# SwiGLU weights split partly by transfers: a negated copy and an adding transfer for the low halves of the output weights, a rounding transfer for the high halves of the up weights

## The chip, the cores and the metric

The kernel runs on one core of a Trainium2 chip. The metric is the device time of one execution in microseconds (us). A core has five engines with instruction queues of their own: TensorE (PE; its weight loads are listed as PEld), VectorE (DVE), ScalarE (ACT), GpSimd (POOL) and SyncE (SP), which here only issues transfers. Each engine takes its instructions in the order of its queue; semaphores order the engines among each other. Sixteen DMA engines move data between DRAM and the on-chip memory.

## The reference

Four layers of a decoder trunk on 512 tokens of 1024 features. Each layer is a token mixer followed by a SwiGLU channel mixer; the change touches the latter alone.

```python
def swiglu(h, w_in, w_out):
    gu = h @ w_in
    return (jax.nn.silu(gu[..., :FFN_HIDDEN]) * gu[..., FFN_HIDDEN:]) @ w_out

for i in range(DEPTH):
    mod = einsum('bd,sde->sbe', silu(c), ada_w[i]) + ada_b[i][:, None, :]
    shift, scale, gate = split(mod, 3, axis=-1)
    ...
    h = x * (1 + scale[1][:, None]) + shift[1][:, None]
    y = swiglu(h, ffn_w_in[i], ffn_w_out[i])
    x = layer_norm(ALPHA * x + (1 + gate[1][:, None]) * y, ln_g[i, 1], ln_b[i, 1])
```

FFN_HIDDEN is 2816, everything is float32. `mod` is the conditioning: columns of scale, shift and gate for each sublayer.

## The kernel before

All activations lie as [feature, token]; a product is a tile of 128 output features by 512 tokens in one bank of PSUM (there are 8 banks). TensorE works in a one-pass format with a shorter mantissa (float32r), so each float32 operand is kept as a high half (the value rounded to that format) and a low half (the rest), and a product is three matmuls: high by high, high by low, low by high (`mm3`, L188 to L190). Tiles of high and low halves of weights are called `wh` and `wl`, those of the modulated input `hh` and `hl`, those of activations `b` in the profile (`b4`, `b2` in the instruction lists).

`weights` brings one tile of weights: SP loads the float32 values into a `raw` tile (L175), ScalarE copies them rounded into `wh` (L178), VectorE writes `wl` = raw - wh (L179). There are five buffers of raw, five of `wh` and five of `wl`. After each weight load, `weights` calls `ada_steps`, which takes one column of the conditioning of a later sublayer from a list: SP loads 512 KB of `ada_w` into a raw tile (L111), VectorE multiplies it with the condition and sums it (L112, one long instruction and a short read of the sum). In a SwiGLU stage the first ten weight loads have no such step (`hold`), and there are 48 of them in each of the first three layers' stages, none in the last.

A SwiGLU stage (`ffn`) goes through the 22 tiles of hidden features in groups of 7, 7 and 8 (FGROUPS). In each group `proj_cols` makes the gate and the up tile of each hidden tile (weights of 512 KB, gate first; the first two hidden tiles of the stage run together in two halves of the tokens), and `gated` makes the activation: silu on ScalarE (L420), times the up tile on VectorE (L421), high half on ScalarE (L422), low half on VectorE (L423). Then `out_proj` multiplies the group's activations with eight output weights (448 KB each, 512 KB in the third group), and `fold` adds each of the eight tiles to the residual `xz` on VectorE (L305). In the third group fold also sums for LayerNorm (L310 to L316), four of its tiles run in two halves of the tokens, and the products that come next begin behind LayerNorm of the first half. `layer_norm` and `modulate` give the next input, with GpSimd computing h (L406). The output projections of the mixers use the same `out_proj`, with two output tiles for each weight load (per = 2); the SwiGLU's have per = 1.

The order on each engine's queue follows from the order in which the program is written and from a scheduler that places each instruction by it; nothing is sorted by hand here.

Of the kernel before, what the change touches and what calls it, by code (L numbers as in the profile page):

```python
# [10 lines left out]
F32 = mybir.dt.float32  # L11
# [3 lines left out]
AF = mybir.ActivationFunctionType  # L15
ALU = mybir.AluOpType
# [3 lines left out]
P = 128  # L20
# [16 lines left out]
# order in which the first input (a) and the first projection (w) are issued  # L37
# [3 lines left out]
class Trunk:  # L41
# [65 lines left out]
    # Output features lie on partitions, so that a product and its sum are one instruction.  # L107
    # They run in steps between the weight loads (see weights()).
# [30 lines left out]
    # The first sublayer's input, one feature tile at a time; its gate comes later.  # L139
# [29 lines left out]
    def weights(self, src, n, eng=None):  # L169
        nc = self.nc  # L170
        raw = self.raw.tile([P, D], F32, tag="raw", name=self.nm("raw"))
        dst = raw[:, :n]
        if len(src.shape) == 3:
            dst = dst.rearrange("p (a b) -> p a b", a=src.shape[1])
        nc.sync.dma_start(dst, src)  # L175
        hi = self.wp.tile([P, D], F32R, tag="wh", name=self.nm("wh"))
        lo = self.wp.tile([P, D], F32R, tag="wl", name=self.nm("wl"))
        nc.scalar.activation(hi[:, :n], raw[:, :n], AF.Copy)  # L178
        (eng or nc.vector).tensor_tensor(lo[:, :n], raw[:, :n], hi[:, :n].bitcast(F32), ALU.subtract)  # L179
        if self.hold:  # L180
            self.hold -= 1
        else:
            self.ada_steps(self.rate)
        return hi, lo
# [17 lines left out]
    def merge(self, *procs):  # L202
        """procs: (generator, total); advances the one that is furthest behind"""
# [10 lines left out]
    def pipeline(self, units, skew):  # L214
        """stage s of unit i comes at step i + skew[s], older units first"""
# [7 lines left out]
    def proj_cols(self, srcs, split, done):  # L223
        """tiles of 128 features: [feature, token]; done(list of banks);
        split: "t" in two halves of the tokens, "k" one input tile at a time"""
        ws = []
        for i, x in enumerate(srcs):
            ws.append(self.weights(x, D, self.nc.gpsimd if split == "k" and i in (1, 3) else None))
            if split == "k":
                yield 0.0  # L230
# [29 lines left out]
    def proj_tok(self, src, n, done):  # L260
        """[token, n features], a bank per 128 tokens; src: [128, 8, n] in DRAM; done(tt, bank)"""
# [24 lines left out]
    def out_proj(self, srcs, per, acts, gate, last):  # L286
        """srcs: one DRAM source for every `per` tiles of 128 output features;
        acts: [128, 2, T] hi/lo tiles. The last group also sums for LayerNorm and
        does `half` of the tiles in two halves of the tokens."""
# [29 lines left out]
        for d0 in range(0, KD - halves, per):  # L319
            w = self.weights(srcs[d0 // per], per * n * P)  # L320
# [5 lines left out]
        if last:  # L326
            ds = list(range(KD - halves, KD))
            ws = {d: self.weights(srcs[d // per], per * n * P) for d in ds[::per]}
# [11 lines left out]
    def layer_norm(self, sub, nxt, half):  # L340
# [3 lines left out]
        # per-token sums as columns, [token, (S1, S2), 2 blocks of tokens]  # L344
# [14 lines left out]
        # back to rows on every partition  # L359
# [32 lines left out]
    # the residual of the next sublayer  # L392
# [17 lines left out]
    def ffn(self, layer, gate):  # L410
        nc, a = self.nc, self.a
        j0 = 0
        for gi, gn in enumerate(FGROUPS):
# [13 lines left out]
            while j < j0 + gn:  # L427
                m = 2 if (gi == 0 and j == 0) else 1
                srcs = [a["ffn_in"][layer, jj, :, x, :] for jj in range(j, j + m) for x in range(2)]
                yield from self.proj_cols(srcs, "t" if m == 2 else None, gated)  # L430
# [7 lines left out]
    def out_srcs(self, w, half):  # L438
        """two output tiles per load, input features of one half"""
# [10 lines left out]
    def transpose_out(self, ytok, n, acts):  # L450
        """ytok: [128 tokens, 4, n*128] -> n hi/lo tiles [128 features, 2, T]"""
# [12 lines left out]
    # x ** -0.5 on a small tile  # L464
# [136 lines left out]
    # 0 where key s <= query t (s on partitions), NEG elsewhere  # L601
# [42 lines left out]
    def rope(self, dst, ps, tt, nh):  # L644
        """dst [128, nh*64] <- rotated ps"""
# [11 lines left out]
    # [keys, queries] masks added to scores: 0 where lo <= q - key < hi, else NEG  # L657
# [254 lines left out]
    def hgrn(self, layer, gate):  # L912
# [79 lines left out]
        def mix(hd):  # L992
# [17 lines left out]
            for l in range(NL + 2):  # L1010
                # K: k times the decay to the end of its block of h, Q: q times the decay
                # from the start of its block, B: the decay over each block
# [92 lines left out]
    def run(self, plan):  # L1105
        """plan: [(kind, layer)] sublayers, sub = 2*layer + (kind == 'ffn')"""
# [5 lines left out]
        for i, (kind, layer) in enumerate(plan):  # L1112
# [15 lines left out]
            # the second half of the tokens is normalised behind the first products  # L1128
# [32 lines left out]
    # alternates so that both end together  # L1161
# [83 lines left out]
```

## Time and profile before

| | |
|---|---|
| median of 2 runs | 2500.31 us (2499.88 to 2500.74) |
| span of the profiled execution | 2498.0 us |
| SwiGLU stages, from and to | 256 to 627, 797 to 1168, 1480 to 1852, 2113 to 2484 us |
| first SwiGLU stage: gate and up tiles | 256 to 339, 378 to 454, 493 to 580 us |
| first SwiGLU stage: output projections | 339 to 378, 454 to 493, 580 to 627 us |

The profile shows one execution. Its span runs from the first to the last instruction; the time of a run is 2.3 us longer than this span. A row of the page's groups reads: line, engine, operation, output and inputs, shapes, count, then busy time and mean of one, then the engine's idle time just before such instructions and what ended it. A row of the list of waits reads: engine, what it wrote and the line, the instruction waited for, then total us, times, the longest. A row of the timeline reads: start, length, engine, line, operation, tiles, and in brackets the idle time before. The landing time of a transfer is counted from its issue to its data being there.

### The profile page before, as it was taken

Reading aid. Unit: us, or ns where it says so; the run is one execution under the profiler, and the core shown is the slowest. Engines: PE = TensorE matmul, PEld = TensorE weight load, DVE = VectorE, ACT = ScalarE, POOL = GpSimd, SP = SyncE. Lnnn points to the kernel's source line nnn. Section 1 sums busy time; section 2 is a strip of 40 time slices with the busy share of each in tenths; the row PEclk is TensorE's granted clock in tenths of the full one; section 3 lists DMA queues with packets and bytes.
Section 4 is the critical chain, followed back from the end, with each engine's and each line's share of the span. In section 5 each row is a group of like instructions: output and inputs, shape, how many; then the busy total and the mean of one; then the engine's idle time right before and its main releaser. Section 6 shows DMA issues by size and latency. Waiting matters only on the chain.

```text
span 2498.0 us, 34328 instructions
## 1 busy us (share of the span) xinstructions
PE 2446.3 (98%) x12920; PEld 2052.5 (82%) x12920; DVE 1432.3 (57%) x2743; ACT 916.6 (37%) x1685; POOL 478.4 (19%) x716
## 2 busy tenths in 40 slices
PE   5999999999999999999999999999999999999998
PEld 4788888888768888889888898888888888888887
DVE  6955765544687655646555566656465556433334
ACT  3433522223653422233433334222345554422223
POOL 7002200003334000104433340000052224000002
PEclk9999999999999999999999999999999999999999
DMA  7842466642211566632222125666422111333331
GB/s 273 287 158 78 132 203 198 198 154 84 77 51 49 171 203 191 206 118 76 77 68 66 63 68 179 205 189 203 119 68 85 60 60 45 109 100 93 101 93 34
DMA packets 93973, 311.94 MB, mean 125 GB/s; under 512 B 10736, under 2 KB 13168, under 8 KB 93808
## 3 DMA queue, kind: packets, MB, share of 16 engines
q1 hardware_dynamic: 92800, 309.43, 38.5%
q8 instruction: 101, 1.65, 0.3%
q10 hardware_dynamic: 1008, 0.32, 0.1%
q14 instruction: 64, 0.52, 0.1%
HBM read 307.62 MB, written 2.10 MB: 124 GB/s over the span
## 4 chain that ended last, share of the span: by engine, by line
PE 89%; DVE 5%; POOL 3%; issue 1%; ACT 1%; DMA 0%; ACTq 0%; POOLq 0%; DVEq 0%
PE ps L188 26%; PE ps L190 26%; PE ps L189 26%; POOL h L406 1%; PE ps L1019 1%; PE ps L853 1%; PE ps L715 1%; DVE wl L179 1%; PE ps L1080 1%; PE ps L881 1%; DVE xz L373 1%; PE ps L746 1%; PE ps L562 1%; DVE xz L381 1%; DVE hl L407 1%
## 5 line engine op out<-in xcount | busy, mean ns | idle before, releaser
L178 ACT ACTIVATE wh<-raw 128x1024 fp32r<-128x1024 f32 (+1 forms) x395 | 410.4, 1042 | 1051.5 <-PE ps L189 652.0
L188 PE MATMUL ps<-hh,wh 128*128 128x512 f32 (+1 forms) x1768 | 655.8, 374 | 19.2 <-ACT wh L178 16.2
L190 PE MATMUL ps<-hh,wl 128*128 128x512 f32 (+1 forms) x1768 | 658.0, 373 | 6.0 <-POOL wl L179 5.1
L189 PE MATMUL ps<-hl,wh 128*128 128x512 f32 (+1 forms) x1768 | 657.4, 373 | 3.7 <-POOL hl L407 3.3
L179 DVE TENSOR_TENSOR wl<-raw,wh 128x1024 fp32r<-128x1024 f32 (+1 forms) x393 | 488.6, 1246 | 284.9 <-ACT wh L178 261.7
L188 PE MATMUL ps<-b,wh 128*128 128x512 f32 (+1 forms) x1216 | 428.0, 352 | 0.0
L189 PE MATMUL ps<-b,wh 128*128 128x512 f32 (+1 forms) x1216 | 421.6, 347 | 0.0
L190 PE MATMUL ps<-b,wl 128*128 128x512 f32 (+1 forms) x1216 | 421.0, 346 | 0.0
L188 PEld LDWEIGHTS ps<-hh,wh 128*128 128x128 f32 x1768 | 333.9, 189 | 76.6 <-ACT wh L178 16.2
L190 PEld LDWEIGHTS ps<-hh,wl 128*128 128x128 f32 x1768 | 334.5, 189 | 65.4 <-POOL wl L179 5.8
L189 PEld LDWEIGHTS ps<-hl,wh 128*128 128x128 f32 x1768 | 334.7, 189 | 64.4 <-POOL hl L407 4.6
L112 DVE CUSTOM_DVE_ANT_0 raw<-raw,cond,adab 128x1024 f32<-128x1024 f32 x192 | 252.2, 1317 | 196.3 <-DMA raw<-in_ada_w 193.2
L188 PEld LDWEIGHTS ps<-b,wh 128*128 128x128 f32 x1216 | 228.7, 188 | 33.4 <-issue 1.2
L189 PEld LDWEIGHTS ps<-b,wh 128*128 128x128 f32 x1216 | 228.6, 188 | 32.9 <-issue 2.0
L190 PEld LDWEIGHTS ps<-b,wl 128*128 128x128 f32 x1216 | 228.5, 188 | 31.0
L305 DVE SCALAR_TENSOR_TENSOR xz<-ps,gate,xz 128x512 f32<-128x512 f32 (+1 forms) x208 | 129.8, 625 | 193.0 <-PE ps L190 192.5
L188 PE MATMUL ps<-wh,hh 128*128 128x512 f32 (+1 forms) x608 | 237.4, 393 | 2.5 <-ACT wh L178 1.5
L189 PE MATMUL ps<-wl,hh 128*128 128x512 f32 (+1 forms) x608 | 221.5, 364 | 0.6 <-DVE wl L179 0.6
L190 PE MATMUL ps<-wh,hl 128*128 128x512 f32 (+1 forms) x608 | 221.6, 365 | 0.0
L421 DVE TENSOR_TENSOR b<-ps,b 128x512 f32<-128x512 f32 x88 | 60.4, 690 | 142.0 <-PE ps L190 139.1
L188 PEld LDWEIGHTS ps<-wh,hh 128*128 128x128 f32 x608 | 115.0, 189 | 23.4 <-issue 3.2
L189 PEld LDWEIGHTS ps<-wl,hh 128*128 128x128 f32 x608 | 115.1, 189 | 19.6 <-DVE wl L179 2.2
(253 smaller groups left out, 2384.1 us busy)
## 6 DMA issues: line engine op xcount, KB each, us to landing
raw<-in_ada_w SPq DMA_DIRECT2D x192, 512.0 KB, 4.1
raw<-in_ffn_in SPq DMA_DIRECT2D x176, 512.0 KB, 3.6
raw<-in_ffn_out SPq DMA_DIRECT2D x64, 448.0 KB, 3.4
raw<-in_ffn_out SPq DMA_DIRECT2D x32, 512.0 KB, 3.5
raw<-in_m_vo SPq DMA_DIRECT2D x16, 512.0 KB, 5.2
raw<-in_h_qf SPq DMA_DIRECT2D x16, 512.0 KB, 3.3
raw<-in_h_ig SPq DMA_DIRECT2D x16, 512.0 KB, 3.9
raw<-in_d_qk SPq DMA_DIRECT2D x16, 512.0 KB, 3.9
```

The source lines that it names most:

```text
L112: self.nc.vector.tensor_tensor_reduce(w, w, self.cond, 1.0, self.adab[:, sub, j : j + 1], ALU.mult, ALU.add, mod[:, j : j + 1])
L178: nc.scalar.activation(hi[:, :n], raw[:, :n], AF.Copy)
L179: (eng or nc.vector).tensor_tensor(lo[:, :n], raw[:, :n], hi[:, :n].bitcast(F32), ALU.subtract)
L188: nc.tensor.matmul(ps, lhs[0], rhs[0], start=start, stop=False)
L189: nc.tensor.matmul(ps, lhs[0], rhs[1], start=False, stop=False)
L190: nc.tensor.matmul(ps, lhs[1], rhs[0], start=False, stop=stop)
L305: nc.vector.scalar_tensor_tensor(z, ps[:, t], gate[:, d : d + 1], z, ALU.mult, ALU.add)
L373: V.tensor_tensor(z, z, st[:, 0, :], ALU.subtract)
L381: V.tensor_tensor(z, z, st[:, 1, :], ALU.mult)
L406: nc.gpsimd.tensor_scalar(h, z, hs[:, k : k + 1], hb[:, k : k + 1], ALU.mult, ALU.add)
L407: (eng or nc.vector).tensor_tensor(self.hl[:, k, t], h, self.hh[:, k, t].bitcast(F32), ALU.subtract)
L421: nc.vector.tensor_tensor(s, pu, s, ALU.mult)
```

## The change

`weights` gets a parameter `how`. With "cast" (the up weights, every second one of `proj_cols` in `ffn`) the high half is written by a transfer that GpSimd issues straight from DRAM, rounding on its way, instead of by ScalarE; raw is still loaded and VectorE still subtracts. With "add" (the output weights of the SwiGLU) ScalarE makes the high half as before, then writes the negated, rounded value into `wl`, and a transfer issued by GpSimd adds the float32 weights from DRAM to it; VectorE's subtraction is gone. There are 88 weights of the first kind (22 hidden tiles, 4 layers) and 96 of the second (64 of 448 KB, 32 of 512 KB). The rest of the diff takes comments out and moves line numbers by 9 from there on.

```diff
-    def weights(self, src, n, eng=None):
+    def weights(self, src, n, eng=None, how=None):
...
-        nc.scalar.activation(hi[:, :n], raw[:, :n], AF.Copy)
-        (eng or nc.vector).tensor_tensor(lo[:, :n], raw[:, :n], hi[:, :n].bitcast(F32), ALU.subtract)
+        if how == "cast":
+            nc.gpsimd.dma_start(hi[:, :n], src)
+        else:
+            nc.scalar.activation(hi[:, :n], raw[:, :n], AF.Copy)
+        if how == "add":
+            nc.scalar.activation(lo[:, :n], raw[:, :n], AF.Copy, scale=-1.0)
+            nc.gpsimd.dma_start(lo[:, :n], src, accum_op=ALU.add)
+        else:
+            (eng or nc.vector).tensor_tensor(lo[:, :n], raw[:, :n], hi[:, :n].bitcast(F32), ALU.subtract)
...
-    def proj_cols(self, srcs, split, done):
+    def proj_cols(self, srcs, split, done, how=None):
...
-            ws.append(self.weights(x, D, self.nc.gpsimd if split == "k" and i in (1, 3) else None))
+            eng = self.nc.gpsimd if split == "k" and i in (1, 3) else None
+            ws.append(self.weights(x, D, eng, how if i % 2 else None))
...
-            w = self.weights(srcs[d0 // per], per * n * P)
+            w = self.weights(srcs[d0 // per], per * n * P, how="add" if per == 1 else None)
...
-            ws = {d: self.weights(srcs[d // per], per * n * P) for d in ds[::per]}
+            ws = {d: self.weights(srcs[d // per], per * n * P, how="add" if per == 1 else None) for d in ds[::per]}
...
-                yield from self.proj_cols(srcs, "t" if m == 2 else None, gated)
+                yield from self.proj_cols(srcs, "t" if m == 2 else None, gated, "cast")
```

In the new numbering the rounding transfer is L180, the high half on ScalarE L182, the negated copy L184, the adding transfer L185 and the subtraction L187. Numbers behind a tile's name count tiles and instructions and differ between the two programs.

GpSimd's queue where the first SwiGLU stage begins, before; sq and S belong to the sums for LayerNorm, lnv is its reciprocal root, h the next input.

```order
L310 TENSOR_SCALAR S_93<-xz_90 128x256
L316 TENSOR_TENSOR S_93<-S_93,sq_334_1909 128x256
L466 TENSOR_TENSOR lnv_337_1919<-lnv_337_1919,mhalf_101 128x2
L316 TENSOR_TENSOR S_93<-S_93,sq_339_1939 128x256
L316 TENSOR_TENSOR S_93<-S_93,sq_341_1957 128x256
L406 TENSOR_SCALAR h_343_1970<-xz_90,hs_303_1706,hb_304_1707 128x256
L316 TENSOR_TENSOR S_93<-S_93,sq_345_1988 128x256
L406 TENSOR_SCALAR h_346_1994<-xz_90,hs_303_1706,hb_304_1707 128x256
```

And after; wh_365 and wh_371 are the stage's first two up weights.

```order
L319 TENSOR_SCALAR S_93<-xz_90 128x256
L180 DMA wh_365_2096<-in_ffn_in 128x1024
L325 TENSOR_TENSOR S_93<-S_93,sq_334_1909 128x256
L475 TENSOR_TENSOR lnv_337_1919<-lnv_337_1919,mhalf_101 128x2
L325 TENSOR_TENSOR S_93<-S_93,sq_339_1939 128x256
L325 TENSOR_TENSOR S_93<-S_93,sq_341_1957 128x256
L415 TENSOR_SCALAR h_343_1970<-xz_90,hs_303_1706,hb_304_1707 128x256
L180 DMA wh_371_2108<-in_ffn_in 128x1024
L325 TENSOR_TENSOR S_93<-S_93,sq_345_1988 128x256
L415 TENSOR_SCALAR h_346_1994<-xz_90,hs_303_1706,hb_304_1707 128x256
```

The two rounding transfers stand between the sums and the tiles of h; each waits there until TensorE has released its buffer.

VectorE's queue at the turn from the gate and up tiles of the first group to its output projection, before; b4_445 is the group's last activation, the L112 rows are conditioning steps.

```order
L112 ISA raw_480_2943,mod_359_2086<-raw_480_2943,cond_94,adab_97 128x1024
L112 ISA mod_359_2086 128x1
L421 TENSOR_TENSOR b2_446_2740<-ps_444_2690,b2_446_2740 128x512
L179 TENSOR_TENSOR wl_469_2876<-raw_467_2873,wh_468_2875 128x896
L423 TENSOR_TENSOR b4_445_2739<-b2_446_2740,b4_445_2739 128x512
L112 ISA raw_485_2975,mod_359_2086<-raw_485_2975,cond_94,adab_97 128x1024
L112 ISA mod_359_2086 128x1
L305 SCALAR_TENSOR_TENSOR xz_90<-ps_451_2754,gate_302_1705,xz_90 128x512
L179 TENSOR_TENSOR wl_474_2908<-raw_472_2905,wh_473_2907 128x896
L112 ISA raw_490_3007,mod_359_2086<-raw_490_3007,cond_94,adab_97 128x1024
L112 ISA mod_359_2086 128x1
```

And after, where the fold is L314.

```order
L112 ISA raw_480_2950,mod_359_2086<-raw_480_2950,cond_94,adab_97 128x1024
L112 ISA mod_359_2086 128x1
L430 TENSOR_TENSOR b2_446_2740<-ps_444_2690,b2_446_2740 128x512
L112 ISA raw_485_2983,mod_359_2086<-raw_485_2983,cond_94,adab_97 128x1024
L112 ISA mod_359_2086 128x1
L432 TENSOR_TENSOR b4_445_2739<-b2_446_2740,b4_445_2739 128x512
L314 SCALAR_TENSOR_TENSOR xz_90<-ps_451_2755,gate_302_1705,xz_90 128x512
L112 ISA raw_490_3015,mod_359_2086<-raw_490_3015,cond_94,adab_97 128x1024
L112 ISA mod_359_2086 128x1
L314 SCALAR_TENSOR_TENSOR xz_90<-ps_456_2788,gate_302_1705,xz_90 128x512
```

The subtractions for the output weights are gone, and the conditioning step on raw_485 now stands ahead of the last activation's low half (L432, before L423) instead of behind it.

ScalarE's queue at the same turn, before.

```order
L178 ACTIVATE wh_463_2843<-raw_462_2841 128x896
L420 ACTIVATE b2_446_2740<-ps_443_2689 128x512
L178 ACTIVATE wh_468_2875<-raw_467_2873 128x896
L422 ACTIVATE b4_445_2739<-b2_446_2740 128x512
L178 ACTIVATE wh_473_2907<-raw_472_2905 128x896
```

And after.

```order
L182 ACTIVATE wh_463_2846<-raw_462_2844 128x896
L429 ACTIVATE b2_446_2740<-ps_443_2689 128x512
L184 ACTIVATE wl_464_2847<-raw_462_2844 128x896
L182 ACTIVATE wh_468_2879<-raw_467_2877 128x896
L184 ACTIVATE wl_469_2880<-raw_467_2877 128x896
L431 ACTIVATE b4_445_2739<-b2_446_2740 128x512
L182 ACTIVATE wh_473_2912<-raw_472_2910 128x896
L184 ACTIVATE wl_474_2913<-raw_472_2910 128x896
```

Behind each high half of an output weight stands the negated copy of the same weight; two of these copies (wl_464, wl_469) now stand ahead of the last activation's high half (L431, before L422). The orders of SP's queue are the same in both, a weight load and a conditioning load in turns, and TensorE's differ only in a few places just behind the start of each SwiGLU stage.

## The prediction, made before the changed kernel was run

> **What bounds the kernel now.** I read the page from the top: the busy line, the slices, and the chain that ended last.
>
> ```profile
> span 2498.0 us, 34328 instructions
> PE 2446.3 (98%) x12920; PEld 2052.5 (82%) x12920; DVE 1432.3 (57%) x2743; ACT 916.6 (37%) x1685; POOL 478.4 (19%) x716
> DMA  7842466642211566632222125666422111333331
> PE 89%; DVE 5%; POOL 3%; issue 1%; ACT 1%; DMA 0%; ACTq 0%; POOLq 0%; DVEq 0%
> ```
>
> TensorE is busy for 98% of the span and carries 89% of the chain. VectorE, from which the change takes most, is busy 57% and carries 5%. Next the waits of TensorE, and what each SwiGLU stage holds (length; then PE, PEld, DVE, ACT and POOL busy with their counts; clock, share of the 16 DMA engines, GB/s).
>
> ```profile
> PE ps L188 <- ACT wh L178: 17.7, 3, 16.2
> PE ps L190 <- POOL wl L179: 5.1, 1, 5.1
> 256.00:627.00 371.00, 369.45 (x1812) 311.15 (x1811) 214.90 (x319) 116.04 (x154) 37.53 (x47) 1.00 0.52 162
> 797.00:1168.00 371.00, 370.12 (x1810) 312.43 (x1809) 217.11 (x322) 116.83 (x153) 50.84 (x81) 1.00 0.51 162
> 1480.00:1852.00 372.00, 370.47 (x1816) 312.08 (x1816) 216.52 (x312) 117.33 (x155) 36.28 (x46) 1.00 0.51 162
> 2113.00:2484.00 371.00, 369.21 (x1811) 311.13 (x1809) 151.18 (x209) 112.57 (x149) 29.57 (x34) 1.00 0.27 85
> ```
>
> The two largest waits hold single pieces of 16.2 and 5.1 us; they are the first projection of the program, which the change leaves alone. In the four stages that it touches TensorE lacks 1.55, 0.88, 1.53 and 1.79 us of the stage's length, 5.8 us in all. That is the most that any gain can bring. What can be lost is not bounded by such a row, so the rest is about losses. The clock is 1.00 throughout and the same matmuls stay, so I let it out of the sum.
>
> **The change, part by part.** Means by form (count | busy, mean ns | idle before, releaser):
>
> ```profile
> L178 ACT ACTIVATE wh<-raw 128x1024 fp32r<-128x1024 f32 x331 | 349.3, 1059 | 811.5 <-PE ps L189 511.0 <-issue 227.8 <-PE ps L190 43.6
> L178 ACT ACTIVATE wh<-raw 128x896 fp32r<-128x896 f32 x64 | 61.0, 954 | 240.1 <-PE ps L189 141.0 <-issue 99.1
> L179 DVE TENSOR_TENSOR wl<-raw,wh 128x1024 fp32r<-128x1024 f32 x329 | 418.8, 1276 | 248.8 <-ACT wh L178 227.6 <-PE ps L190 18.0
> L179 DVE TENSOR_TENSOR wl<-raw,wh 128x896 fp32r<-128x896 f32 x64 | 69.8, 1091 | 36.1 <-ACT wh L178 34.1
> L112 DVE CUSTOM_DVE_ANT_0 raw<-raw,cond,adab 128x1024 f32<-128x1024 f32 x192 | 252.2, 1317 | 196.3 <-DMA raw<-in_ada_w 193.2
> ```
>
> *Arithmetic.* VectorE loses the low halves of the 96 output weights: 64 x 1.091 + 32 x 1.276 = 110.7 us. ScalarE loses the high halves of the 88 up weights, 88 x 1.059 = 93.2, and gains 96 negated copies, 64 x 0.954 + 32 x 1.059 = 94.9: no change. Neither sets the end here. ScalarE's copies wait for TensorE to give buffers back (511.0 us of idle time before them), that is, weights stand ready. All this is worth 0.
>
> *Transfers.* GpSimd issues 184 more, 88 x 512 + 64 x 448 + 32 x 512 KB, about 90 MB. What the engines now carry (same columns as the stages; 339 to 378 is an output projection, 378 to 454 the gate and up tiles behind it, 2196 to 2235 the same projection in the last layer, which loads no conditioning):
>
> ```profile
> 339.00:378.00 39.00, 39.00 (x168) 31.37 (x168) 23.82 (x31) 8.55 (x10) 1.81 (x4) 1.00 0.65 203
> 378.00:454.00 76.00, 76.00 (x337) 62.91 (x336) 43.79 (x57) 21.22 (x28) 0.23 (x1) 1.00 0.63 194
> 2196.00:2235.00 39.00, 39.00 (x170) 31.58 (x169) 15.89 (x18) 8.75 (x10) 0.00 (x0) 1.00 0.32 108
> ```
>
> Eight plain loads of 448 KB cost 0.32 x 39 = 12.5 us of the DMA engines, 1.56 each. With eight adding ones at the plain price the loaded projection goes from 0.65 to 0.97. TensorE's pace is 39 / 8 = 4.88 us an output weight and 76 / 14 = 5.43 an input weight, and with five buffers a new one has 4 x 4.88 = 19.5 us. The longer way of a low half (two copies of 0.954, then issue and transfer) leaves the last two 17.6 us. So a single added transfer is hidden; what it does to its neighbours need not be.
>
> *The chain of conditioning loads.* In these stages SP alternates weight load and conditioning load. Each conditioning load waits until VectorE's L112 is done with the previous one, and L112 stands in VectorE's queue between the folds and the activations. Three rows of that instruction (the 1st, 8th and 23rd from there on), the end of one and the load issued on it, the landing times in the windows 338:378 and 378:454, and the median landings of other loads (KB, us):
>
> ```profile
> 341.36 1.28 DVE L112 CUSTOM_DVE_ANT_0 raw<-raw,cond,adab 128x1024 f32<-128x1024 f32 x1
> 378.32 1.28 DVE L112 CUSTOM_DVE_ANT_0 raw<-raw,cond,adab 128x1024 f32<-128x1024 f32 x1 [1.83 <-DMA raw<-in_ada_w]
> 457.04 1.28 DVE L112 CUSTOM_DVE_ANT_0 raw<-raw,cond,adab 128x1024 f32<-128x1024 f32 x1 [0.37 <-DMA raw<-in_ada_w]
> 529.86 1.28 DVE L112 CUSTOM_DVE_ANT_0 raw<-raw,cond,adab 128x1024 f32<-128x1024 f32 x1 [1.05 <-DMA raw<-in_ada_w]
> 338.02 0.08 DVE L112 DVE_READ_ACCUMULATOR2_ANT mod<- 128x1 f32 x1
> 338.13 0.33 SPq L111 DMA_DIRECT2D raw<-in_ada_w  x1
> DMA to landing us min/median/max: 3.2/3.5/4.4
> DMA to landing us min/median/max: 3.3/3.8/4.4
> raw<-in_ffn_in SPq DMA_DIRECT2D x176, 512.0 KB, 3.6
> raw<-in_m_vo SPq DMA_DIRECT2D x16, 512.0 KB, 5.2
> ```
>
> In the projection a step of this chain takes (378.32 - 341.36) / 7 = 5.28 us: 3.5 landing, 1.36 for L112 and its read, 0.42 between. TensorE needs 4.88 a step, so VectorE falls 8 x 0.40 = 3.2 us behind. In the next fourteen steps it takes (457.04 - 378.32) / 15 = 5.25 against 5.43 and makes 14 x 0.18 = 2.5 us good. The chain is level with TensorE by a hair, and whatever lengthens a landing is added to each step.
>
> All three transfers of a step are released by the same event, the end of an output tile on TensorE (the fold, then L112 and the next conditioning load; the two copies, then the weight load and the adding transfer), so they share the DMA engines. At the plain price an adding transfer puts between nothing and its whole 1.56 us ahead of the conditioning load; I take the middle, 0.8, so 3.5 becomes 4.3 and the step 6.08: 8 x (6.08 - 4.88) = 9.6 us behind. In the input stage every other step has a rounding transfer of 1.56 x 512 / 448 = 1.8 us; half of it every second step is 0.45, and the step between 5.25 (hidden in waits for TensorE) and 5.70: between 2.5 us made good and 3.8 lost; I take the middle, 0.6 lost.
>
> Where TensorE meets it is the next turn from gate and up to output projection. There L112 now stands ahead of the last activation's low half:
>
> ```profile
> 340.61 0.68 DVE L423 TENSOR_TENSOR b<-b,b 128x512 fp32r<-128x512 f32 x1
> 343.02 0.39 PE L189 MATMUL ps<-b,wh 128*128 128x512 f32 x1
> ```
>
> That half was done at 341.29 and is needed at 343.02. Behind L112 (341.36 + 1.36 + 0.68) it is done at 343.40: 0.4 us late at the first turn, with nothing else changed. At the second turn it is late by 0.4 + 9.6 + 0.6 less the 0.4 already waited: 10.2. At the third the conditioning has ended (last L112 at 529.86, turn at 580), and VectorE has caught up. So 10.6 us a layer, and three layers load conditioning: 31.8 us. Ends: 3 x 0.4 = 1.2 (no landing grows) and 3 x (8 x 1.96 + 3.8 + 0.4) = 60 (all of a plain transfer in front).
>
> *Start of each SwiGLU stage.* The second up weight of the stage gets its buffer late, and its high half now needs a transfer where a copy stood:
>
> ```profile
> 253.24 1.06 ACT L178 ACTIVATE wh<-raw 128x1024 fp32r<-128x1024 f32 x1 [0.26 <-PE ps L189]
> 256.93 0.28 PE L188 MATMUL ps<-hh,wh 128*128 128x256 f32 x1
> 248.90 0.83 POOL L466 TENSOR_TENSOR lnv<-lnv,mhalf 128x2 f32<-128x2 f32 x1
> 253.06 0.73 POOL L316 TENSOR_TENSOR S<-S,sq 128x256 f32<-128x256 f32 x1 [0.36 <-ACT sq L314]
> ```
>
> From 253.24 to 256.93 are 3.69 us. The trace has no transfer issued by GpSimd; its instruction on two columns, 0.83, is the nearest row for a fixed cost, and the landing is 3.6: 0.74 us late, 4 x 0.74 = 3.0 us for four layers. Ends: 0, and with 5.2 for the landing 4 x 2.34 = 9.4. Behind this issue GpSimd's queue holds a sum for LayerNorm (here 253.06) and the next tiles of h; with 0.8 us for the issue they move by less than they idle. The Trainium skill ("DMA: Bandwidth & Descriptors", Latency and other measured facts) gives about 1 us to the first byte on GpSimd's path and 0.6 on SP's; by this estimate the delay would be 0.4 instead of 0.83 and the term 1.2 us; no run so far shows it.
>
> Sum: 2498.0 + 31.8 + 3.0 = 2532.8 us of span. The median of the runs, 2500.31, lies 2.3 us above the profiled span; with it 2535 us.
>
> **The rivals.** *Hidden* (no landing grows): 2498.0 + 1.2 + 3.0 + 2.3 = 2504 to 2505. For it: in the projection landings spread only from 3.2 to 4.4 at a share of 0.65. Against it: the share goes to 0.97.
>
> *The adding transfer costs twice a plain one or more* (other side of the line). It must read what it adds to. At 3.12 us each, half in front makes the landing 5.06 and the step 6.84: 3 x (15.7 + 0.6 + 0.4) = 50 us, 2553; all in front, 6.62 and 8.40: 3 x (28.2 + 3.8 + 0.4) = 97, 2600; the middle is 2577. The projection would then need 25.4 + 25 us of the DMA engines in 39, so they fall behind too. The line of 2%, 2550, is crossed when the landing in the projection reaches 4.95 us instead of 3.5. For it: 5.2 us under the load of the start, where the slices show 7 and 8 tenths. Against it: there many loads stand in one queue, here three. The Trainium skill ("Collectives: The Full Stack", Part 3: Why 7× under link rate — side-by-side accounting) has such a rule: an add in the DMA issues two source reads for each chunk where a copy issues one, on the same ring, and ran at 1/1.93 of the rate; no trace here holds an adding transfer, so it stays open.
>
> *Faster:* at most 5.8 us of idle time, 2494 to 2498, and only if VectorE's missing 110.7 us were waited for; the waits of TensorE show no such place.
>
> *It does not do what it says:* if the rounding transfer copies without rounding, the low half is zero and the time is the same.
>
> **How the numbers follow.** Forecast (chain of conditioning loads grows at about the plain price) 0.46, hidden 0.16, adding transfer at twice or more 0.36, faster 0.02. 2% of 2500 is 50 us, about what a measurement of this kernel can tell from no change. Faster by over 2% is excluded by the idle time: 0.01 for what I overlook. Slower: 0.36 and 0.05 from the upper end of the forecast: 0.41. Within: 0.58. The range runs from the hidden case, 2503, to the twofold price all in front, 2605, leaving out some 0.05 below and 0.13 above. The forecast's own is 2504 to 2565 (3 x 0.4 to 60 us in the chain).
>
> **What would show it.** L112 steps between the first and second turn at about 6.1 us instead of 5.28, landings of conditioning in the projections near 4.3, and waits of TensorE for the last activation's low half (some 10 us, three times, at the second turn). Waits for an up weight's transfer near 0.7 us at the start of the stages. VectorE about 111 us less busy, ScalarE the same. It is wrong if TensorE waits for low halves of output weights or if the last layer, which loads no conditioning, grows by more than about 1 us: then the transfers themselves are the cause.

## The result, and the profile after

| | before | after |
|---|---|---|
| median | 2500.31 us | 2634.14 us (2633.40 to 2634.89, 2 runs) |
| span of the profiled execution | 2498.0 us | 2631.7 us |
| ratio of the runs | | 1.0531, 95% interval 1.0512 to 1.0549 |

The changed kernel is 5.3% slower; the forecast was 2535 us, range 2503 to 2605. The page of the changed kernel (busy line, slices, DMA queues, chain):

```profile
span 2631.7 us, 34559 instructions
PE 2469.3 (94%) x12920; PEld 2063.5 (78%) x12920; DVE 1315.8 (50%) x2647; ACT 908.1 (35%) x1693; POOL 592.5 (23%) x900
PEclk9999989899999989799999999898999999999999
DMA  7832576767211676776222226867672211475653
q1 hardware_dynamic: 92800, 309.43, 36.1%
q0 software_dynamic: 26496, 92.29, 15.9%
PE 75%; DMA 10%; DVE 7%; issue 4%; POOL 3%; ACT 1%; DVEq 0%; POOLq 0%; SPq 0%; ACTq 0%
```

VectorE is 116.5 us less busy, ScalarE 8.5, and TensorE has the same 12920 matmuls. The chain that ended last now runs for 10% over transfers, which had 0%. The slices show something new for this kernel: the granted clock drops in six of them. The waits of TensorE in the changed kernel (total us, times, longest):

```profile
PE ps L196 <- ACT b L431: 66.3, 9, 11.7
PE ps L197 <- DVE b L432: 36.4, 9, 4.9
PE ps L196 <- ACT wh L182: 19.9, 3, 18.3
PE ps L197 <- POOL hl L416: 5.4, 3, 2.8
PE ps L196 <- ACT hh L412: 4.5, 6, 0.9
PE ps L196 <- DMA wh<-in_ffn_in: 3.7, 4, 1.0
```

The first two, 102.7 us, were not in the list of before: TensorE waits for the high and low halves of a group's last activations. The sixth is the up weight at the start of each SwiGLU stage. The same by stages of the first layer (length; PE, PEld, DVE, ACT, POOL busy; clock, DMA share, GB/s), the two loaded projections, and the same projection in the last layer, which loads no conditioning:

```profile
341.00:396.00 55.00, 42.14 (x170) 33.23 (x169) 19.68 (x28) 11.73 (x14) 6.37 (x11) 0.88 0.78 212
474.00:537.00 63.00, 42.09 (x169) 32.55 (x168) 22.24 (x33) 12.86 (x16) 5.90 (x8) 0.81 0.78 212
2329.00:2368.00 39.00, 39.00 (x170) 31.61 (x169) 10.44 (x13) 9.81 (x11) 4.57 (x6) 1.00 0.77 182
```

The projections took 39 us each. With conditioning they take 55 and 63, of which TensorE is busy 42 at a lower clock; without it 39, with the same adding transfers and the same share of the DMA engines. Where the 133.7 us of span went: 102.7 in those waits, 23.0 in matmuls that took longer (2469.3 against 2446.3 busy), 3.7 at the starts of the stages; 4.3 net are left in other waits, of which none grew by more than 2.2.

How it comes about is read from the timeline. VectorE in the first layer of the changed kernel, up to the first turn (the first and the twelfth conditioning step, what stands around them), and the two waits of TensorE there:

```profile
299.18 1.23 DVE L187 TENSOR_TENSOR wl<-raw,wh 128x1024 fp32r<-128x1024 f32 x1 [3.83 <-issue]
300.32 1.28 DVE L112 CUSTOM_DVE_ANT_0 raw<-raw,cond,adab 128x1024 f32<-128x1024 f32 x1
350.97 1.28 DVE L112 CUSTOM_DVE_ANT_0 raw<-raw,cond,adab 128x1024 f32<-128x1024 f32 x1 [6.11 <-DMA raw<-in_ada_w]
352.18 0.69 DVE L430 TENSOR_TENSOR b<-ps,b 128x512 f32<-128x512 f32 x1
357.25 1.28 DVE L112 CUSTOM_DVE_ANT_0 raw<-raw,cond,adab 128x1024 f32<-128x1024 f32 x1 [4.38 <-DMA raw<-in_ada_w]
358.46 0.69 DVE L432 TENSOR_TENSOR b<-b,b 128x512 fp32r<-128x512 f32 x1
353.58 0.80 PE L196 MATMUL ps<-b,wh 128*128 128x512 f32 x1 [8.04 <-ACT b L431]
359.20 0.79 PE L197 MATMUL ps<-b,wh 128*128 128x512 f32 x1 [4.82 <-DVE b L432]
```

L430 and L432 make the last activation. Each has a conditioning step ahead of it, and VectorE stands in front of that step for 6.11 and 4.38 us until its load has landed. TensorE then waits 8.04 us for the high half and 4.82 for the low one. Only the step ahead of L432 is there through the change. The one ahead of L430 stood there before as well, and its row and that of L421, which makes the same tile, show that it was done in time, with VectorE waiting for TensorE and not the other way round:

```profile
336.81 1.29 DVE L112 CUSTOM_DVE_ANT_0 raw<-raw,cond,adab 128x1024 f32<-128x1024 f32 x1 [1.56 <-DMA raw<-in_ada_w]
338.86 0.69 DVE L421 TENSOR_TENSOR b<-ps,b 128x512 f32<-128x512 f32 x1 [0.76 <-PE ps L190]
```

So the greater part of the wait, 66.3 us of 102.7, is for the high half, behind a step that the change did not move but made late.

### The profile page after: what moved, and what is told of

The parts are those of the page before. It is cut to its first block, busy times and chain, and to the rows that moved or that the text cites. A ratio compares the mean times of both kernels' runs of the same rounds, so it can differ in the third digit from the quotient of the medians.

```text
span 2631.7 us, 34559 instructions
## 1 busy us (share of the span) xinstructions
PE 2469.3 (94%) x12920; PEld 2063.5 (78%) x12920; DVE 1315.8 (50%) x2647; ACT 908.1 (35%) x1693; POOL 592.5 (23%) x900
## 3 DMA queue, kind: packets, MB, share of 16 engines
q1 hardware_dynamic: 92800, 309.43, 36.1%
q0 software_dynamic: 26496, 92.29, 15.9%
## 4 chain that ended last, share of the span: by engine, by line
PE 75%; DMA 10%; DVE 7%; issue 4%; POOL 3%; ACT 1%; DVEq 0%; POOLq 0%; SPq 0%; ACTq 0%
PE ps L197 22%; PE ps L198 22%; PE ps L196 22%; DMA raw<-in_ada_w 9%; DVE raw L112 2%; DVE wl L187 2%; POOL h L415 1%; PE ps L1028 1%; PE ps L862 1%; PE ps L724 1%; PE ps L1089 1%; PE ps L890 1%; DVE xz L382 1%; PE ps L755 1%; PE ps L571 1%
## 5 line engine op out<-in xcount | busy, mean ns | idle before, releaser
L182 ACT ACTIVATE wh<-raw 128x1024 fp32r<-128x1024 f32 (+1 forms) x307 | 316.6, 1035 | 697.6 <-PE ps L197 415.1
L196 PE MATMUL ps<-b,wh 128*128 128x512 f32 (+1 forms) x1216 | 436.5, 359 | 66.3 <-ACT b L431 66.3
L187 DVE TENSOR_TENSOR wl<-raw,wh 128x1024 fp32r<-128x1024 f32 x297 | 369.6, 1248 | 248.0 <-issue 103.1
L112 DVE CUSTOM_DVE_ANT_0 raw<-raw,cond,adab 128x1024 f32<-128x1024 f32 x192 | 252.2, 1317 | 453.7 <-DMA raw<-in_ada_w 453.6
L197 PE MATMUL ps<-b,wh 128*128 128x512 f32 (+1 forms) x1216 | 429.6, 353 | 36.4 <-DVE b L432 36.4
L198 PE MATMUL ps<-b,wl 128*128 128x512 f32 (+1 forms) x1216 | 427.2, 351 | 0.0
L196 PEld LDWEIGHTS ps<-b,wh 128*128 128x128 f32 x1216 | 233.0, 192 | 105.1 <-ACT b L431 71.1
L197 PEld LDWEIGHTS ps<-b,wh 128*128 128x128 f32 x1216 | 232.8, 191 | 74.4 <-DVE b L432 41.0
L314 DVE SCALAR_TENSOR_TENSOR xz<-ps,gate,xz 128x512 f32<-128x512 f32 (+1 forms) x208 | 129.9, 626 | 224.8 <-PE ps L198 224.2
L185 POOL DMA_DIRECT2D wl<-in_ffn_out x96 | 83.4, 869 | 516.7 <-ACT wl L184 489.8
L431 ACT ACTIVATE b<-b 128x512 fp32r<-128x512 f32 x88 | 54.9, 629 | 412.3 <-DVE b L430 412.3
L180 POOL DMA_DIRECT2D wh<-in_ffn_in x88 | 49.3, 560 | 578.8 <-PE ps L198 496.6
```

The costliest lines, as they stand in the source:

```text
L112: self.nc.vector.tensor_tensor_reduce(w, w, self.cond, 1.0, self.adab[:, sub, j : j + 1], ALU.mult, ALU.add, mod[:, j : j + 1])
L180: nc.gpsimd.dma_start(hi[:, :n], src)
L185: nc.gpsimd.dma_start(lo[:, :n], src, accum_op=ALU.add)
L196: nc.tensor.matmul(ps, lhs[0], rhs[0], start=start, stop=False)
L197: nc.tensor.matmul(ps, lhs[0], rhs[1], start=False, stop=False)
L198: nc.tensor.matmul(ps, lhs[1], rhs[0], start=False, stop=stop)
```

## The experiments

Theory A is the forecast's mechanism, with the sizes open: the new transfers lengthen the landing of the conditioning loads; each such load is issued only behind the step on the one before; VectorE's queue stands behind the steps, and the last activations behind VectorE. Theory B: the order alone, the step ahead of the last activation. Theory C: the rounding transfers.

| run | median, us | ratio to before, 95% interval | TensorE waits for last activations, us |
|---|---|---|---|
| rounding transfers alone | 2554.03 | 1.0210 (1.0177 to 1.0242) | 31.5 |
| adding transfers alone | 2561.82 | 1.0241 (1.0202 to 1.0279) | 48.5 |
| order alone, GpSimd subtracts | 2521.14 | 1.0074 (1.0054 to 1.0095) | 7.6 |
| two buffers for conditioning | 2599.55 | 1.0392 (1.0361 to 1.0422) | 41.0 |
| old order, adding beside it | 2663.88 | 1.0652 (1.0621 to 1.0683) | 125.2 |
| old order, no adding beside it | 2557.59 | 1.0227 (1.0197 to 1.0257) | 38.1 |
| sixth raw buffer | 2645.30 | 1.0577 (1.0555 to 1.0599) | 108.2 |
| sixth buffer, step one later | 2645.68 | 1.0579 (1.0562 to 1.0596) | 106.9 |
| the same edits on the kernel before | 2498.59 | 0.9989 (0.9980 to 0.9999) | 0 |
| step on the weight tile | 2609.69 | 1.0434 (1.0383 to 1.0485) | 85.5 |
| raw buffers in pairs | 2573.97 | 1.0291 (1.0253 to 1.0329) | 42.7 |
| no conditioning in the SwiGLU stages | 2509.02 | 1.0024 (1.0012 to 1.0037) | 0 |

**One part of the change at a time.** Rounding alone takes `how="add"` out, adding alone takes "cast" out.

```diff
-            w = self.weights(srcs[d0 // per], per * n * P, how="add" if per == 1 else None)
+            w = self.weights(srcs[d0 // per], per * n * P)
...
```

> The rounding transfers alone; the output weights are split as in the kernel before. Theory A (the three to four transfers at a turn lengthen the landing of the conditioning loads, VectorE's queue waits behind them, TensorE waits for the last activations): no adding transfer stands at the turns, so 2503 to 2525 us, with the 3.7 us of waits for up weights at the stage starts. Theory B (the order alone: the conditioning step ahead of the last activation): 2503 to 2510. Theory C (the rounding transfers cause it): over 2580.

```diff
-                yield from self.proj_cols(srcs, "t" if m == 2 else None, gated, "cast")
+                yield from self.proj_cols(srcs, "t" if m == 2 else None, gated)
```

> The adding transfers alone; the up weights are split as in the kernel before. Theory A: most of the loss, 2580 to 2635 us, waits of TensorE for L431 and L432 over 60 us. Theory B: the whole 131 us. Theory C: under 2525.

Neither came out as expected. Rounding alone, from which I expected next to nothing, costs 2.1%; adding alone costs 2.4%, less than "most of the loss". Together they cost more than the sum. The first and the twelfth conditioning step of the first layer show that they act in two places. With rounding alone:

```profile
298.01 1.23 DVE L187 TENSOR_TENSOR wl<-raw,wh 128x1024 fp32r<-128x1024 f32 x1 [3.29 <-issue]
299.16 1.28 DVE L112 CUSTOM_DVE_ANT_0 raw<-raw,cond,adab 128x1024 f32<-128x1024 f32 x1
349.41 1.28 DVE L112 CUSTOM_DVE_ANT_0 raw<-raw,cond,adab 128x1024 f32<-128x1024 f32 x1 [1.04 <-DMA raw<-in_ada_w]
```

With adding alone:

```profile
295.38 1.28 DVE L112 CUSTOM_DVE_ANT_0 raw<-raw,cond,adab 128x1024 f32<-128x1024 f32 x1
352.66 1.28 DVE L112 CUSTOM_DVE_ANT_0 raw<-raw,cond,adab 128x1024 f32<-128x1024 f32 x1 [3.28 <-DMA raw<-in_ada_w]
```

And the kernel before (its twelfth step is the one at 341.36 in the prediction):

```profile
293.36 1.27 DVE L112 CUSTOM_DVE_ANT_0 raw<-raw,cond,adab 128x1024 f32<-128x1024 f32 x1
```

| | first step | eleven steps | each | twelfth step |
|---|---|---|---|---|
| before | 293.36 | 48.00 | 4.36 | 341.36 |
| rounding alone | 299.16 | 50.25 | 4.57 | 349.41 |
| adding alone | 295.38 | 57.28 | 5.21 | 352.66 |
| both | 300.32 | 56.93 | 5.18 | 357.25 |

Rounding starts the steps 5.8 us late and slows each by 0.2. Adding slows each by 0.85; nearly all of the 2.0 us by which its first step is later lies ahead of the stage, where a subtraction at 227.26 in the kernel before stands at 229.12 with adding alone, at 227.51 with rounding alone and at 228.36 with both. With both, late start and slower steps come together. The late start stands behind L187, a subtraction ahead of the first step in the queue: with both, GpSimd issued the rounding transfer for that up weight at 292.47 and L187 began at 299.18, where before ScalarE's copy took 1.06 us.

**The order alone.** VectorE's queue as in the changed kernel at the turns, no added transfer: GpSimd subtracts for the output weights, and the rounding transfers are taken out as in the run with adding alone.

```diff
-            nc.scalar.activation(lo[:, :n], raw[:, :n], AF.Copy, scale=-1.0)
-            nc.gpsimd.dma_start(lo[:, :n], src, accum_op=ALU.add)
+            nc.gpsimd.tensor_tensor(lo[:, :n], raw[:, :n], hi[:, :n].bitcast(F32), ALU.subtract)
...
```

> VectorE's order as in the changed kernel (the conditioning step ahead of the last activation, no subtraction for output weights), without any added transfer: the low halves of the output weights are subtracted by GpSimd. Theory A: landings stay at 3.5 to 3.8 us, some 0.4 to 2 us lost at a turn, 2500 to 2512 us. Theory B: most of the loss, over 2580.

The waits of TensorE in this run:

```profile
PE ps L196 <- DVE b L431: 7.6, 6, 1.5
```

Six turns, 1.3 us each, and the profiled span is 2507.3. The median of six runs is higher, 2521 (2509 to 2525); the profiled run and one other, at 2509 and 2512, show a mean granted clock of 0.997, those at 2519 to 2525 one of 0.991 to 0.995. So the bound that I gave, 2512, was too tight; theory B as the cause of most of the loss falls.

**Giving the conditioning its own buffers.**

```diff
-        self.raw = pool("raw", 5)
+        self.raw = pool("raw", 4)
...
-        w = self.raw.tile([P, D], F32, tag="raw", name=self.nm("raw"))
+        w = self.raw.tile([P, D], F32, tag="araw", name=self.nm("araw"), bufs=2)
```

> The changed kernel with two raw buffers of their own for the conditioning loads and four for the weights, so that a conditioning load need not wait for the step before it (the scheduler then also places the conditioning further ahead). Theory A: the landings may stay long, but the waits of TensorE for L431 and L432 fall from 103 us to under 30, time 2500 to 2540. A theory that the adding transfers themselves come late for TensorE: unchanged, about 2630.

A miss: 2600 us. The scheduler placed the conditioning far ahead, so that it also stands among the mixers' work; the waits for the last activations stay in the first two layers, and there are none in the third, whose conditioning was done by then. The edit changed more than the thing it was to test.

**The old order with the new traffic.** The kernel before, and for each output weight a negated copy into one spare tile and a transfer onto it.

```diff
+        if how == "add":
+            x = self.scr.tile([P, D], F32R, tag="scr", name=self.nm("scr"))
+            nc.scalar.activation(x[:, :n], raw[:, :n], AF.Copy, scale=-1.0)
+            nc.gpsimd.dma_start(x[:, :n], src, accum_op=ALU.add)
...
```

> The kernel before with the new traffic beside it: for each output weight of the SwiGLU a negated copy into a spare tile and an adding transfer into that, which nothing reads; VectorE's subtractions and its order stay. Theory A (landing times): landings of conditioning 4.3 to 5 us in the output projections and a loss of 20 to 130 us by waits for the last activations, though the step on the turn stands behind the last activation. Theory B (order): 2500 to 2510.

The other run leaves `accum_op` out (the spare tile is in the rounded format, so this transfer rounds).

> As the one before, with a plain transfer instead of the adding one. If adding costs more than moving, the share of the DMA engines in the last layer's output projections (0.32 before) rises to about 0.64 here and to 0.77 with adding, and the loss is smaller: theory A 2500 to 2560. Theory B: 2500 to 2510.

These do not decide. There is one spare tile, so that ScalarE waited for the transfer before: 300.3 us with adding, 166.9 without, in a queue that also makes the activations. With adding even the last layer lost 5 to 8 us at each turn, which the changed kernel does not. Only one thing can be read from the second: with conditioning TensorE waited at the first two turns of three layers, in the last layer not at all, as in the changed kernel.

**More slack for the load, one buffer more.**

```diff
-        self.raw = pool("raw", 5)
+        self.raw = pool("raw", 6)
```

> The changed kernel with a sixth raw buffer and nothing else; VectorE's queue keeps its order at the turns. Theory A in the form that the chain of load, step, next load is what is too slow: the next conditioning load can be issued before the step on the one before is done, so the steps follow each other faster and the waits for L431 and L432 (103 us) fall by half or more, 2505 to 2560 us. If the place of the step in VectorE's queue alone counts, or the transfers come late for TensorE by themselves: 2620 to 2640.

The second run also lets each step work on the load of the step before.

```diff
         self.nc.sync.dma_start(w, self.a["ada_w"][sub, j])
+        self.ada_flush()
+        self.pend = (w, mod, sub, j)
...
```

> The changed kernel with a sixth raw buffer, and each conditioning step working on the load of the step before, so that a landing has one step (about 5 us) more; every transfer stays, and VectorE's queue has its steps at the same places. Theory A (VectorE stands behind a landing): waits for L431 and L432 under 15 us, the clock at 1.00, 2500 to 2520 us. Without theory A (the DMA engines are too full, or an adding transfer is late for TensorE): over 2590.

> The control: the kernel before with the same two edits, without the new transfers. Theory A and any other: 2496 to 2503, since TensorE idles only 5.8 us in these stages.

The control came out as expected, a tenth of a per cent below the kernel before; the other two missed, at 2645 us. What SP's conditioning loads waited for says why; in the changed kernel, with the sixth buffer, and in the run with the later step:

```profile
SPq L111 <- DVE mod L112: 470.0, 129, 8.3
```

```profile
SPq L111 <- DVE mod L112: 478.8, 130, 8.7
```

```profile
SPq L111 <- DVE mod L122: 475.9, 129, 8.2
```

As before, each conditioning load is issued when the step before has ended: the conditioning loads still take turns in a single buffer, and the sixth did not go to them. The slack that the edit was to give was not there.

**The step on another tile, and buffers in pairs.** In the first the step takes the weight tile that was just loaded.

```diff
-            w, w, self.cond, 1.0, self.adab[:, sub, j : j + 1], ALU.mult, ALU.add, mod[:, j : j + 1]
+            self.junk[:, :m], x, self.cond[:, :m], 1.0, self.adab[:, sub, j : j + 1], ALU.mult, ALU.add, mod[:, j : j + 1]
...
+            self.last = raw[:, :n] if self.infn else None
```

> The changed kernel with all its transfers, the conditioning loads too, but in the SwiGLU stages each conditioning step works on the weight tile that has just been loaded instead of on its own load, which nothing reads (so the conditioning columns of these stages are not computed). VectorE's queue has its steps nearly at the same places; it no longer waits for the landing of a load issued only after the step before. The two runs with a sixth raw buffer did not test this: the buffer went to the weights, SP still issued each conditioning load behind the step before. Theory A: waits for L431 and L432 (103 us) under 20, 2500 to 2525 us, though the share of the DMA engines is no smaller. If full DMA engines or late adding transfers hold TensorE by themselves: over 2590.

A miss of theory A's number, 2610. Two views tell why, SP's waits and VectorE's:

```profile
SPq L180 <- DMA raw<-in_ada_w: 540.1, 117, 8.5
```

```profile
DVE junk L116 <- DMA raw<-in_ffn_in: 280.2, 87, 8.9
DVE junk L116 <- DMA raw<-in_ffn_out: 166.6, 42, 7.7
```

A load nobody reads still holds the one buffer until it has landed; SP's next weight load stands behind that, and VectorE now waits for the weight. One landing a step, as before, under another name. So this run tests neither theory A nor full DMA engines.

In the other, a raw buffer has two halves, one for the weight and one for the conditioning load beside it, three in rotation.

```diff
-        self.raw = pool("raw", 5)
+        self.raw = pool("raw", 3)
...
+            pair = self.raw.tile([P, 2, D], F32, tag="raw", name=self.nm("raw"))
+            raw = pair[:, 0, :]
...
```

> The changed kernel with three raw buffers of two halves, one for the weight and one for the conditioning load that goes with it, so that a conditioning load waits for the step three before it, not for the last one; everything is computed. Theory A, chain of load and step: the steps come at TensorE's pace again, waits for L431 and L432 under 40 us, 2500 to 2560. Otherwise 2620 or more.

2574 us. SP's waits and TensorE's in this run:

```profile
SPq L115 <- DVE mod L116: 63.9, 17, 11.1
```

```profile
PE ps L204 <- DVE b L439: 29.4, 8, 5.8
PE ps L203 <- ACT b L438: 13.3, 5, 5.9
```

Here the loads no longer wait for the step before (63.9 us instead of 470.0), with every transfer in place and everything computed. TensorE's waits fall from 102.7 to 42.7 us and 60 of 134 us come back, short of what I expected (under 40, and at most 2560). The matmuls take as long as in the changed kernel, 2470.2 us against 2469.3. The landing of the conditioning loads is longer now, a median of 6.1 us over the program against 4.6 in the changed kernel.

**No conditioning in the three stages.**

```diff
+        if self.infn:
+            self.nc.vector.memset(mod[:, j : j + 1], 0.0)
+            return
...
```

> The changed kernel with both kinds of transfers, without the 144 conditioning loads and steps that fall into the first three SwiGLU stages (their columns are set to zero). The run in which the step worked on the weight tile did not take the wait away: VectorE then waited for the landing of the weight, which SP issued behind the conditioning load. Theory A: without conditioning the three stages take 371 to 374 us each, as the last layer's does with the change, waits for L431 and L432 under 5 us, 2498 to 2510. If rounding and adding transfers cost by themselves: over 2550.

2509.0 us, 0.24% over before, as theory A had it. The first three parts of the first layer's SwiGLU stage (gate and up tiles, output projection, gate and up tiles) and the wait of TensorE that is new against before:

```profile
257.00:341.00 84.00, 81.90 (x448) 71.46 (x447) 40.68 (x100) 35.85 (x53) 20.62 (x32) 0.98 0.51 145
341.00:380.00 39.00, 39.00 (x169) 31.40 (x168) 11.12 (x13) 9.84 (x11) 4.59 (x6) 1.00 0.76 183
380.00:456.00 76.00, 76.00 (x337) 62.93 (x336) 21.19 (x24) 19.80 (x26) 6.15 (x9) 1.00 0.53 149
```

```profile
PE ps L199 <- DMA wh<-in_ffn_in: 4.0, 4, 1.1
```

The projection is at 39 us with a DMA share of 0.76, and of all the waits that the change brought, those for the first up weights are left. Without conditioning beside them the rounding and adding transfers cost 0.24%; in the profile these waits are 4.0 us of it, and longer matmuls 2.9 (2449.2 against 2446.3 busy). The rest of the loss needs the conditioning. This run takes out its loads and its steps together, so it does not say which of the two it is.

## Why the prediction was wrong

The mechanism was right in kind, its size in the waits at the turns by more than a factor of three too small, and one term was left out. The measured time lies above the range and above the dear rival's 2600.

- **The bound on a gain and the arithmetic: right.** VectorE's missing 116.5 us (forecast 110.7) bought nothing, and without conditioning the change costs 0.24%. ScalarE, forecast to stay the same, is 8.5 us less busy, which does not bear on the end.
- **The start of each stage: right in the sum, in part by luck.** Forecast 3.0 us, measured 3.7 for four waits. In the first layer the rounding transfer is issued at 254.95, behind a tile of h in GpSimd's queue, 1.7 us after the time at which the copy began before, while the stage itself is 0.9 late; it lands 3.9 us after its issue, where the sum had 0.83 + 3.6. The two differences nearly cancel.
- **The second and third turn, the last layer: right in kind.** TensorE waits at the second turn, not at the third; the last layer takes 39 us for the same projection as before, and its one new wait is the 0.88 us at its start.
- **"0.4 us late at the first turn, with nothing else changed": the step that failed.** It waits 8.04 + 4.82 = 12.9 us in the first layer. The prediction left the steps ahead of the turn as they were, and there the change had already acted twice. The twelfth step is 357.25 - 341.36 = 15.9 us later: 7.0 from the late start (1.1 of it from ahead of the stage), 11 x 0.81 = 8.9 from slower steps. TensorE reached the turn 2.6 us later (341.2 against 338.6). Three of the projection's eight adding transfers are issued before the turn, at 321.51, 331.37 and 333.05, and 7.9 of the 8.9 us arise from the sixth step on, which begins at 320.63. I had costed the rounding transfers at the start of the stage and by their share of the DMA engines, not by what stands behind the subtraction that waits for them in VectorE's queue. The prediction also counted only the low half, behind the step that the change moved; 8.04 of the 12.9 us are for the high half, behind the step that had been there. Even the 0.4 was too small: with the order alone the first turns cost 1.2 to 1.5 us.
- **The second turn: right place, half the size.** 10.2 us forecast, 7.00 + 3.36 + 6.07 + 4.47 = 20.9 measured in the first layer; from the twelfth to the 34th step the chain takes (498.81 - 357.25) / 22 = 6.43 us a step, and before (457.04 - 341.36) / 22 = 5.26. The forecast's steps average (8 x 6.08 + 14 x 5.47) / 22 = 5.69. The median landing of a conditioning load, forecast at 4.3 instead of 3.5, is 4.8 in the first loaded projection (341 to 396) and 4.9 in the second (474 to 537). The 34th step, VectorE in the changed kernel:

```profile
498.81 1.28 DVE L112 CUSTOM_DVE_ANT_0 raw<-raw,cond,adab 128x1024 f32<-128x1024 f32 x1 [4.03 <-DMA raw<-in_ada_w]
```

  Both turns give 33.8 us a layer instead of 10.6, and 102.7 in all instead of 31.8.
- **"The same matmuls stay, so I let it out of the sum": wrong.** The same matmuls took 23.0 us more, since the clock did not stay at 1.00: 0.88 and 0.81 in the two loaded projections, where TensorE waited, and 1.00 in the last layer's. Around the first turn of the changed kernel (same columns as the stages, clock third from the end):

```profile
337.00:341.00 4.00, 4.00 (x20) 3.30 (x19) 2.11 (x4) 0.88 (x2) 0.00 (x0) 1.00 1.00 247
350.00:364.00 14.00, 5.60 (x13) 4.08 (x14) 5.83 (x9) 2.42 (x3) 0.86 (x1) 0.51 0.63 190
364.00:374.00 10.00, 10.00 (x45) 8.05 (x44) 2.71 (x4) 3.59 (x4) 1.14 (x2) 1.00 0.89 205
```

  At 350 to 364, behind the first long wait and through the second, the clock is 0.51; then 1.00 again. The Trainium skill ("TensorE: Matmul & The Clock Gate", Part 1: The HAM clock gate (the "warmup" mystery)) lets the clock fall to one half after an idle window of about 3.4 us and return after about as long a busy one. The profiled runs agree with it for the waits at the turns: those of at most 1.5 us (the order alone) cost no clock, those of 3 to 12 us in the changed kernel did. They do not agree everywhere: in the run without conditioning the clock is 0.53 and 0.61 from 266 to 268 and 268 to 270, where no wait since 256 was longer than 0.94 us. I had not weighed the clock.
- **The price of the adding transfer: the rival was nearer.** From the queues of the run with adding alone and its span of 2564.1 us (queue, packets, MB, share):

```profile
q1 hardware_dynamic: 92800, 309.43, 37.9%
q0 software_dynamic: 13824, 46.14, 10.3%
```

  The adding queue took 0.103 x 2564.1 / 46.14 = 5.72 us for a MB, the loads 0.379 x 2564.1 / 309.43 = 3.14, a ratio of 1.82. The Trainium skill ("Collectives: The Full Stack", Part 3: Why 7× under link rate — side-by-side accounting) has 1/1.93 of the rate for an add; this run agrees within 6%. TensorE does not stand behind adding transfers: none of its waits in the changed kernel is for one. But how far full engines lengthen the landings stays open. They are full for a while (1.00 at 337 to 341, above), and 0.78 of the 55 us of the first loaded projection are 42.9 us of transfers, more than the 39 us that it took before; without conditioning they are 0.76 x 39 = 29.6. The rival would also have missed, as it took the same 0.4 for the first turn.

The three terms, 102.7 + 23.0 + 3.7 = 129.4 of 133.7 us, are read from the profile, each as a difference to before. That the conditioning's place beside the new transfers is the cause of the loss is shown by the runs without conditioning and with buffers in pairs. With the pairs, which break the turns of load and step and leave every transfer, 60 us of the waits go; 42.7 and the slower clock stay. How these divide between landings that full DMA engines lengthen and what the queues pass on (VectorE's step holds ScalarE's copies, these hold SP's loads) was not separated: no run took the load off the engines and left the queues as they were.

## What to carry to other kernels

A transfer that is itself hidden can be dear through a neighbour: look for loads that wait for an instruction that waits for the load before (one buffer in turns), and ask how much longer each landing may get before that loop is slower than the engine it feeds; here it had 5.28 against 4.88 us in the projections, no room at all. Count such a loop from its first turn, not from the place where the new work is used, and look which in-order queue stands behind each of its steps. When a forecast lets TensorE wait in pieces of several microseconds, its clock belongs in the sum.

## What the runs showed of the hardware that was not expected

- The clock's part does not follow the sum of the waits. Busy time of the same 12920 matmuls against waits for the last activations: 2446.3 us with none (before), 2446.4 with 7.6 us in pieces up to 1.5 (order alone), 2459.9 with 31.5 (rounding alone), 2462.0 with 48.5 (adding alone), 2469.3 with 102.7 (both); but 2470.2 with only 42.7 (pairs) and 2474.3 with 41.0 (two buffers for conditioning).
- GpSimd's rounding transfers take hardly more of the DMA engines than plain loads: in the run with rounding alone (span 2549.1) 5.9% for 46.14 MB against 37.7% for 309.43, 3.26 and 3.11 us a MB. The adding ones take 1.82 times as much as loads, and land later (changed kernel, median from issue); without conditioning beside them it is still 7.2 us, against 3.4 for a load of the same size:

```profile
wh<-in_ffn_in POOLq DMA_DIRECT2D x88, 512.0 KB, 5.0
raw<-in_ffn_out SPq DMA_DIRECT2D x64, 448.0 KB, 4.4
wl<-in_ffn_out POOLq DMA_DIRECT2D x64, 448.0 KB, 7.3
```

- The issue of one adding transfer holds GpSimd for 0.87 us and that of a rounding one for 0.56 (groups of the changed kernel), where the prediction had taken 0.83 for a rounding one from a row of before:

```profile
L185 POOL DMA_DIRECT2D wl<-in_ffn_out x96 | 83.4, 869 | 516.7 <-ACT wl L184 489.8
L180 POOL DMA_DIRECT2D wh<-in_ffn_in x88 | 49.3, 560 | 578.8 <-PE ps L198 496.6
```
